# The quadrant sums of W_out in a Winograd feed-forward layer: formed during FFN-out on GpSimd, or during FFN-in on VectorE

## The chip, the cores and the metric

The kernel runs on one core of one Trainium2 chip. The core has a matrix engine (TensorE, in the profile PE, with PEld for its weight loads), VectorE (DVE), ScalarE (ACT), GpSimd (POOL) and SyncE (SP, which only issues transfers here), and 16 DMA engines. Engines run their own instruction streams in order and wait for each other on semaphores. SBUF is the on-chip memory of 128 partitions, PSUM holds what TensorE writes, and DRAM tensors keep what does not fit. The metric is the device time of one execution in microseconds (us), lower is better. A kernel is timed in several runs, and the median counts.

## The reference

One layer of an encoder trunk over 1024 tokens of width 1024, in float32:

```
h = swiglu(rms_norm(x), ffn1_w_in, ffn1_w_out);  x = x + 0.5 * rms_norm(h)
m = token_mixing(rms_norm(x), ...);              x = x + rms_norm(m)
h = swiglu(rms_norm(x), ffn2_w_in, ffn2_w_out);  x = x + 0.5 * rms_norm(h)

def _swiglu(x, w_in, w_out):
    g, u = jnp.split(x @ w_in, 2, axis=-1)      # w_in: 1024 x 5632
    return (jax.nn.silu(g) * u) @ w_out         # w_out: 2816 x 1024
```

Token mixing is a projection, a retention branch and a neighbourhood attention, and three output projections. The change touches the two feed-forward layers, above all the product with `w_out`.

## The kernel before

**Exact float32 from three passes.** Each operand is split into a high part (ScalarE, line 61) and the rest (VectorE, or GpSimd where asked, line 62), and `mm3` (lines 88 to 90) makes three matmuls of a 128x128 by a 128x512 tile: high by high, rest by high, high by rest. So an operand tile of 128x512 needs one ScalarE and one VectorE instruction before TensorE can use it. `piece` splits into a ring of eight wh/wl pairs; `raw` loads 512 KB into the ring `wraw` of three buffers of 4 KB a partition.

**Winograd.** Every large product is cut into 2x2 quadrants and done with seven products in place of eight (`Winograd`, `Pairs`). That needs sums of quadrants of the operands. For the left operand they are called a11, a12, a22, s1 to s4. For the right operand b they are t1 = b12 - b11, t2 = b22 - t1, t3 = b22 - b12 and t4 = b21 - t2.

**FFN-in** (`ffn_in`, `Pairs.run`). 22 pairs of column tiles; one pair is seven products of 12 matmuls. VectorE makes the t sums of the pair's weights, the rests of the splits, the additions of the products out of PSUM and the gate product (line 417); ScalarE makes the high parts and SiLU. After every second pair `LeftFactors` forms the left factors of the following product on GpSimd (line 440), and stores all seven to DRAM tensors `g0...` or `g1...` by GpSimd's DMA queue (`store`, line 68). Six (first layer) or four (second) pairs have two of their seven products done ahead (`lead`); in the first layer three of them wait in six buffers with the tag `lead`.

**FFN-out** (`ffn_out`). Seven products, in the order a11, s1, s2, s3, a22, a12, s4, of 11 steps each. A step takes one 128x512 tile of the left factor (`Blocks`: load `graw`, split into gh and gl) and one of the right operand, and makes 12 matmuls: four token tiles of 128 by three passes. Four PSUM banks gather a product and are taken out by p1 to p7. The left factors sit in two pools, g0 and g1, with four buffers of gh and gl in all.

The right operand is whole in SBUF: twelve tiles `x` of up to four 128x512 blocks hold the four quadrants of `w_out`, loaded on SyncE's queue at the steps of `LOADS`. GpSimd forms the t sums in place, one block at a time (`sub`, line 537; `prepare` puts t1 from step 8, t2 from 19, t3 from 24 and t4, which forms t2 anew, from 30). That is 55 subtractions in each FFN-out. The first four blocks of b11 come as raw loads instead.

After the fourth product GpSimd adds q tiles (lines 571, 572) and ScalarE takes their squares (line 481) for the post-norm. Tokens 0 to 511 are finished during the last two products, tokens 512 to 1023 after them. The residual tiles `xs` are loaded into freed blocks of the quadrants, those of tokens 512 to 1023 of the first layer into the wraw ring (`xload`).

**Between the stages.** The first FFN-out passes its rows to the mixer's projection: norm, transposes on TensorE, and the sums of the next left operand in `Winograd.put`. The mixer's loads and the attention (pools pa, na, ret) follow.

**Order.** Instructions are written in the order of the program; the framework schedules them per engine by that order as priority and puts the waits in. Pools are opened and closed by stage on two stacks, left and right, in SBUF. A pool that lands on bytes of closed pools waits for all of their users before any of its tiles can be used. The scratch for the descriptors of GpSimd's DMA queue has its default size.

Of the kernel before, what the change touches and what calls it, by code (L numbers as in the profile page):

```python
# [10 lines left out]
F32 = mybir.dt.float32  # L11
# [21 lines left out]
LOADS = (0, 2, 4, 6, 9, 12, 14, 17, 20, 23, 26, 29)  # L33
# [371 lines left out]
def ffn_in(c, pairs, pool, put):  # L405

    nc = c.nc
    for i in range(FT):
        gate = [pool.tile([P, 512], F32, tag=f"c{j}", name=f"c{j}", bufs=2) for j in range(2)]
        gt = pool.tile([P, S], F32, tag="gt", name="gt", bufs=3)  # L410
        up = gt[:, :512], gt[:, 512:]

        def done(j):
            if j < 2:
                nc.scalar.activation(gate[j], gate[j], AF.Silu)  # L415
            if j in (1, 2):
                nc.vector.tensor_tensor(up[j % 2], gate[j % 2], up[j % 2], ALU.mult)  # L417
        pairs.run(i, (*gate, *up).__getitem__, done)
        put(i, gt)
# [87 lines left out]
def ffn_out(c, tiles, q, blocks, w_out, gl, ep, side={}):  # L507
# [5 lines left out]
    spare = [t[2][:, 3] for b in tiles for t in b]  # L513
    later, rest, flips, xs = [], [], [], {}

    def quad(k, i, j):
        return tiles[i][j][k // 4][:, k % 4]

    def load(i, j, n):
        m = min(4, NK - 4 * n)  # L520
        nc.sync.dma_start(tiles[i][j][n][:, :m], w_out[2 * i + j][:, n * 2048:n * 2048 + m * 512]
                          .rearrange("p (k f) -> p k f", k=m))

    def xload(t):

        if t < 4 or ep.pre is None:
            tile = (tiles[0][1] + tiles[0][0])[t // 2]
            xs[t] = tile[:, t % 2 * 2:t % 2 * 2 + 2].rearrange("p k f -> p (k f)")
            nc.sync.dma_start(xs[t], ep.resid(t))
        else:  # L530
            xs[t] = c.raw(ep.resid(t))


    order = []

    def sub(out, a, b):
        e = nc.gpsimd.tensor_tensor(out, a, b, ALU.subtract).ins  # L537
        if order:
            c.tc.add_manual_dep(e, order[-1].name, mybir.DependencyInfo(
                mybir.DependencyClass.NoSync, mybir.DependencyReason.DATA), reason="order")  # L540
        order.append(e)

    def t1(k):
        sub(quad(k, 0, 0), quad(k, 0, 1), quad(k, 0, 0))

    def t2(k):
        sub(spare[k % 4], quad(k, 1, 1), quad(k, 0, 0))

    def t3(k):
        sub(quad(k, 0, 1), quad(k, 1, 1), quad(k, 0, 1))  # L550

    def t4(k):
        t2(k)
        sub(quad(k, 0, 0), quad(k, 1, 0), spare[k % 4])
# [11 lines left out]
    def p7(u, b):  # L566
        tt(q[3][:, u], b, q[1][:, u], ALU.add)

        def more():
            xload(u)  # L570
            add(q[1][:, u], q[1][:, u], q[2][:, u], ALU.add)
            add(q[2][:, u], q[3][:, u], q[2][:, u], ALU.add)
            ep.square(u, 1, q[2][:, u], spare[u])
        later.extend((more, None))
# [17 lines left out]
    def p3(u, b):  # L592
        e = tt(q[1][:, u], b, q[1][:, u], ALU.add)
        out = q[1][:, u] if ep.pre is not None else q[3][:, u]
        ep.square(4 + u, 1, q[1][:, u], b if ep.pre is not None else spare[2 + u % 2], out, nc.vector if u == 3 else nc.gpsimd)
# [10 lines left out]
        if u == 2 and 7 not in xs:  # L606
            xload(7)

    def b11(k):
        if k < 4:  # L610
            if k % 2 == 0:
                raws.append(c.raw(w_out[0][:, k * 512:(k + 2) * 512]))
            return raws[-1][:, k % 2 * 512:k % 2 * 512 + 512]
        return quad(k, 0, 0)

    raws = []
    products = (("a11", b11, p1), ("s1", lambda k: quad(k, 0, 0), p5),
                ("s2", lambda k: spare[k % 4], p6), ("s3", lambda k: quad(k, 0, 1), p7),
                ("a22", lambda k: quad(k, 0, 0), p4), ("a12", lambda k: quad(k, 1, 0), p2),
                ("s4", lambda k: quad(k, 1, 1), p3))  # L620
    steps = [(i, k) for i in range(len(products)) for k in range(NK)]
    loads = dict(zip(LOADS, ((0, 0, 1), (0, 0, 2), (0, 0, 0),
                             *((i, j, n) for i, j in ((0, 1), (1, 1), (1, 0)) for n in range(3)))))
    xloads = {n: 4 + j for j, n in enumerate((68, 69, 70) if ep.pre is not None else (59, 62, 65, 68))}
    operands, banks, last = {}, {}, []

    def prepare(n):
        for f, n0 in zip((t1, t2, t3, t4), (8, 19, 24, 30)):
            if 0 <= n - n0 < NK:
                f(n - n0)  # L630
# [9 lines left out]
    for n, (i, k) in enumerate(steps):  # L640
        for m in range(2):
            operand(n + m)
        if n in loads:
            load(*loads[n])
        prepare(n)
# [380 lines left out]
def trunk_layer(ctx: ExitStack, tc, x, g1a, w1i, w1o, g1b, gma, wmt, wnv, wrv, logits, dtab, rope, bias,  # L1026
# [15 lines left out]
    gl = [{n: dt(f"g{i}{n}", [P, FT // 2 * 512]) for n in Winograd.NAMES} for i in range(2)]  # L1042
    x1, x2 = dt("x1", [S, D]), dt("x2", [S, D])
# [13 lines left out]
    def pool(stack, name, side="left"):  # L1057
        return stack.enter_context(tc.tile_pool(name=name, bufs=1, side=side))
# [5 lines left out]
    with tc.tile_pool(name="norm1", bufs=1) as ep:  # L1064
# [10 lines left out]
    g0 = pool(left, "gl10")  # L1075
    with tc.tile_pool(name="fin1", bufs=1) as fp:
        ffn_in(c, fin, fp, LeftFactors(c, early, gl[0]))
    right.close()

    spool = pool(left, "s1")  # L1080
# [3 lines left out]
    wx = Winograd(c, (x0pool, x1pool, spool), None, (4, 4, 2, 8, 8, 8, 8), d["a21"])  # L1084
    ep_stack, g_stack = ExitStack(), ExitStack()
    ep = pool(ep_stack, "ep1")
    g1 = pool(g_stack, "gl11")
    b11, b12, b21, b22 = ([p.tile([P, 4, 512], F32, tag="x", name="x", bufs=n) for p, n in q] for q in (
        ((x0pool, 4),) * 3, ((x1pool, 2), (x1pool, 2), (x0pool, 4)), ((spool, 8),) * 3, ((spool, 8),) * 3))
    q = [p.tile([P, 4, 512], F32, tag="x", name="q", bufs=n) for p, n in ((ep, 2), (ep, 2), (spool, 8), (spool, 8))]  # L1090
    ahead = {}
    fo = Epilogue(c, ep, g1b, gma, rows(x), rows(x1), wx.put)
    rest = ffn_out(c, [[b11, b12], [b21, b22]], q, Blocks(c, (g0, g1, g1, g1), (1, 3)), w1o, gl[0], fo,
                   {n: (lambda j=j: ahead.update({j: c.load_w(wnv[j])})) for j, n in enumerate((65, 66))})
    g_stack.close()
    wx.tmp = pool(g_stack, "cmb1")
# [61 lines left out]
    with tc.tile_pool(name="pa", bufs=1) as pa:  # L1158
# [95 lines left out]
    with tc.tile_pool(name="na", bufs=1) as na:  # L1254
# [3 lines left out]
    with tc.tile_pool(name="ret", bufs=1) as ret:  # L1258
# [50 lines left out]
    with tc.tile_pool(name="ep2", bufs=1) as ep:  # L1309
# [12 lines left out]
    with tc.tile_pool(name="fin2", bufs=1) as fp:  # L1322
        ffn_in(c, fin, fp, LeftFactors(c, cmb, gl[1]))
# [3 lines left out]
    g0, g1, w2 = (pool(right, n, "right") for n in ("gl20", "gl21", "w2"))  # L1327
    tiles = [[[w2.tile([P, 4, 512], F32, tag="x", name="x", bufs=12) for _ in range(3)] for _ in range(2)]
             for _ in range(2)]
    with tc.tile_pool(name="out2", bufs=1) as op:  # L1330
        q = [op.tile([P, 4, 512], F32, tag="q", name="q", bufs=4) for _ in range(4)]
        ffn_out(c, tiles, q, Blocks(c, (g0, g1, g0, g1), (2, 2)), w2o, gl[1],
                Epilogue(c, op, g2b, None, rows(x2), rows(out), None))
# [79 lines left out]
```

## Time and profile before

| what | value |
|---|---|
| time, median of 3 runs | 2327.08 us (2325.92 to 2331.17) |
| span of the profiled execution | 2324.0 us; the page gives no other time of that execution |
| between span and median | 3.1 us |
| TensorE busy | 96% of the span |
| first FFN-in, FFN-out | to 455.4 us; 455.4 to about 692 us |
| second FFN-in, FFN-out | to 2088.0 us; 2088.0 to about 2315 us |

The profile is one execution. A row of a timeline has start, duration, engine, line, operation, output<-input. A row of the groups has line, engine, operation, tiles, shapes, count, then busy us and mean ns of one, then the idle time of the engine just before those instructions and what ended it. A row of the waits says who waited for whom: us in total, times, longest. A row of the chain has start, duration and what ran. A row of the DMA issues has what goes where, the queue, the count, KB of each and the median us from issue to landing. In rows of stretches a pair such as `22.06 (x95)` is busy time and number of instructions. Instructions of VectorE and TensorE overlap a little with the next one, so the distance of two starts is what one takes of the engine's time.

### The profile page before, as it was taken

To read this page: it belongs to the slowest core of one execution; us is meant where nothing else is said; L and a number is where in the kernel's file an instruction comes from. 1 tells how busy PE (TensorE), PEld (TensorE's weight loads), DVE (VectorE), ACT (ScalarE), POOL (GpSimd) and SP (SyncE) were. 2 spreads that over 40 slices of the span, in tenths; PEclk is the share of its full clock that TensorE was granted. 3 is DMA by queue.
4 is the path that set the end of the run, shared out by engine and by line. 5 is a ranking of instruction groups with operands and counts; after the bars stand their busy time and mean duration, and the time that the engine had idled before them with its cause. 6 is when DMAs were issued, how large, how long until landed. Compare 5 with 4: busy or idle time off the path is not lost.

```text
span 2324.0 us, 29917 instructions
## 1 busy us (share of the span) xinstructions
PE 2230.8 (96%) x10288; PEld 1840.8 (79%) x10288; DVE 1742.4 (75%) x2833; ACT 1004.1 (43%) x2102; POOL 744.6 (32%) x735
## 2 busy tenths in 40 slices
PE   6999999999998999999999999999799999999998
PEld 5788888777786887778888888887588888887776
DVE  7886666689778768869875678547887666668966
ACT  6332222343454323248885675226533333224443
POOL 5232222368424134411101222101523131326942
PEclk9999999999998999999999999999899999999999
DMA  4332323374335542257744566766433232328443
GB/s 145 121 137 101 117 95 110 138 275 153 106 114 172 177 159 100 108 177 243 219 164 172 162 219 233 281 219 212 146 114 118 95 114 95 118 92 321 122 130 122
DMA packets 135896, 361.25 MB, mean 155 GB/s; under 512 B 16000, under 2 KB 43776, under 8 KB 133632
## 3 DMA queue, kind: packets, MB, share of 16 engines
q1 hardware_dynamic: 109344, 271.76, 36.1%
q0 software_dynamic: 26400, 87.58, 9.5%
q8 instruction: 81, 1.33, 0.2%
q14 instruction: 71, 0.58, 0.1%
HBM read 263.33 MB, written 100.14 MB: 156 GB/s over the span
## 4 chain that ended last, share of the span: by engine, by line
PE 71%; DVE 13%; issue 7%; POOL 4%; DMA 3%; ACT 3%; POOLq 0%; SPq 0%; DVEq 0%; ACTq 0%
PE ps L90 22%; PE ps L88 22%; PE ps L89 22%; DVE wl L62 3%; DVE gl L62 2%; PE pt L88 1%; PE pt L89 1%; PE pt L90 1%; DMA wraw<-in_dram 1%; DVE tmp L118 1%; POOL rstd L98 1%; DMA x<-in_dram 1%; ACT wh L61 1%; POOL cmb L288 1%; POOL q L482 1%
## 5 line engine op out<-in xcount | busy, mean ns | idle before, releaser
L62 DVE TENSOR_TENSOR wl<-wraw,wh 128x512 fp32r<-128x512 f32 x516 | 381.3, 762 | 80.0 <-ACT wh L61 79.0
L61 ACT CAST wh<-wraw 128x512 fp32r<-128x512 f32 x524 | 300.7, 618 | 205.4 <-PE ps L89 68.2
L90 PE MATMUL ps<-wh,gl 128*128 128x512 f32 x612 | 242.7, 400 | 16.4 <-DVE gl L62 16.0
L88 PE MATMUL ps<-wh,gh 128*128 128x512 f32 x612 | 241.9, 397 | 7.0 <-ACT gh L61 5.8
L89 PE MATMUL ps<-wl,gh 128*128 128x512 f32 x612 | 241.4, 395 | 2.1 <-DVE wl L62 2.1
L62 DVE TENSOR_TENSOR gl<-graw,gh 128x512 fp32r<-128x512 f32 (+2 forms) x178 | 184.3, 1039 | 76.6 <-ACT gh L61 76.4
L61 ACT CAST gh<-graw 128x512 fp32r<-128x512 f32 (+2 forms) x178 | 106.7, 601 | 211.9 <-PE ps L89 68.5
L537 POOL TENSOR_TENSOR x<-x 128x512 f32<-128x512 f32 x110 | 181.0, 1672 | 40.1 <-DMA x<-in_dram 28.9
L415 ACT ACTIVATE c<-c 128x512 f32<-128x512 f32 x88 | 55.7, 633 | 294.7 <-DVE c L385 195.3
L62 DVE TENSOR_TENSOR wl<-x,wh 128x512 fp32r<-128x512 f32 x146 | 168.0, 1161 | 8.2 <-ACT wh L61 8.2
L90 PEld LDWEIGHTS ps<-wh,gl 128*128 128x128 f32 x612 | 116.4, 191 | 51.9 <-DVE gl L62 28.1
L88 PEld LDWEIGHTS ps<-wh,gh 128*128 128x128 f32 x612 | 116.6, 190 | 34.2 <-ACT gh L61 8.9
L89 PEld LDWEIGHTS ps<-wl,gh 128*128 128x128 f32 x612 | 116.8, 191 | 26.9 <-DVE wl L62 3.2
L61 ACT CAST wh<-t 128x512 fp32r<-128x512 f32 x58 | 36.1, 622 | 197.3 <-DVE t L379 196.0
L90 PE MATMUL ps<-a12h,wl 128*128 128x512 f32 x280 | 109.9, 393 | 3.7 <-DVE wl L62 3.7
L88 PE MATMUL ps<-a11h,wh 128*128 128x512 f32 x280 | 111.6, 399 | 1.4 <-ACT wh L61 0.7
L90 PE MATMUL ps<-a11h,wl 128*128 128x512 f32 x280 | 110.5, 395 | 0.7 <-DVE wl L62 0.7
L89 PE MATMUL ps<-a11l,wh 128*128 128x512 f32 x280 | 110.6, 395 | 0.0
L88 PE MATMUL ps<-a12h,wh 128*128 128x512 f32 x280 | 110.3, 394 | 0.0
L68 POOL DMA_DIRECT2D g1a<-gt x33 | 18.1, 550 | 286.3 <-DVE gt L417 286.3
L88 PE MATMUL ps<-a22h,wh 128*128 128x512 f32 x280 | 109.8, 392 | 0.0
L89 PE MATMUL ps<-a12l,wh 128*128 128x512 f32 x280 | 109.2, 390 | 0.0
(359 smaller groups left out, 6197.6 us busy)
## 6 DMA issues: line engine op xcount, KB each, us to landing
wraw<-in_dram SPq DMA_DIRECT2D x221, 512.0 KB, 4.4
x<-in_dram SPq DMA_DIRECT2D x16, 1024.0 KB, 6.9
g0s<-cmb POOLq DMA_DIRECT2D x44, 256.0 KB, 2.5
graw<-g0s SPq DMA_DIRECT2D x44, 256.0 KB, 2.9
g1s<-cmb POOLq DMA_DIRECT2D x44, 256.0 KB, 2.6
graw<-g1s SPq DMA_DIRECT2D x44, 256.0 KB, 3.0
bt<-in_dram SPq DMA_DIRECT2D x24, 384.0 KB, 4.0
g0a<-gt POOLq DMA_DIRECT2D x33, 256.0 KB, 2.3
```

The source lines that it names most:

```text
L61: nc.scalar.copy(h, src)
L62: (eng or nc.vector).tensor_tensor(l, src, hf, ALU.subtract)
L68: self.nc.gpsimd.dma_start(dst, src)
L88: mm(ps, a[0], b[0], start=start, stop=False)
L89: mm(ps, a[0], b[1], start=False, stop=False)
L90: mm(ps, a[1], b[0], start=False, stop=stop)
L98: self.nc.gpsimd.tensor_tensor(r[:, :n], ms, self.mhalf[:, :n], ALU.pow)
L118: nc.vector.scalar_tensor_tensor(xn[:, bs], x[:, bs], r[:, 0:1], gain[:, bs], op0=ALU.mult, op1=ALU.mult)
L288: nc.gpsimd.tensor_tensor(s3, h2, s3, ALU.subtract)
L415: nc.scalar.activation(gate[j], gate[j], AF.Silu)
L482: (eng or c.nc.gpsimd).tensor_tensor(h if out is None else out, h, self.post[:, b * 512:(b + 1) * 512], ALU.mult)
L537: e = nc.gpsimd.tensor_tensor(out, a, b, ALU.subtract).ins
```

## The change

- `OutSums` is new. In FFN-in it loads the four quadrants of `w_out`, one 128x512 block of each, forms t1 to t4 of the block on VectorE and stores them to DRAM tensors `t0...` or `t1...` through GpSimd's queue. `ffn_in` calls it after each of the four results of a pair, from pair 6 (first layer) or 4 (second). The first call of a block issues the loads, the next four one subtraction and one store each: 55 calls for 11 blocks. The buffers are the six of tag `lead` in the first layer, four new ones (`tw`) in the second.
- `ffn_out` has no quadrants in SBUF and no subtractions. `wraw` loads the right operand of two steps at a time, from `w_out` or the stored sums, into the ring `wraw`; the left factors come as before.
- The residual tiles `xs` have buffers of their own and are loaded at steps 30 to 36 and 57 to 63.
- The pools of SBUF named in the diff and all opened by the helper `pool` take `reuse_waits="tile"`: a tile waits only for the users of earlier tiles on its own bytes.
- The pools are laid out anew: in the first FFN-out q, junk, left factors and x tiles lie on the left in the order mid0, gl10, mid1, gl11, mid2, the rest (ep1) on the right; the mixer's pool s1 is opened after them. The scratch for GpSimd's DMA descriptors becomes 4 KB a partition.

```diff
-def ffn_in(c, pairs, pool, put):
+def ffn_in(c, pairs, pool, put, sums):
...
             if j in (1, 2):
                 nc.vector.tensor_tensor(up[j % 2], gate[j % 2], up[j % 2], ALU.mult)
+            sums(i)
...
+class OutSums:
+    def __init__(self, c, tile, src, dst, first):
+        self.first, self.left = first, self.steps(c, tile, src, dst)
+
+    @staticmethod
+    def steps(c, tile, src, dst):
+        tt = c.nc.vector.tensor_tensor
+        for k in range(FT // 2):
+            ks = slice(k * 512, (k + 1) * 512)
+            b11, b12, b21, b22 = b = [tile() for _ in range(4)]
+            for q in range(4):
+                c.nc.sync.dma_start(b[q], src[q][:, ks])
+            yield
+            for n, o, x, y in ((0, b11, b12, b11), (2, b12, b22, b12), (1, b22, b22, b11), (3, b21, b21, b22)):
+                tt(o, x, y, ALU.subtract)
+                c.store(dst[n][:, ks], o)
+                yield
+
+    def __call__(self, i):
+        if i >= self.first:
+            next(self.left, None)
...
-def ffn_out(c, tiles, q, blocks, w_out, gl, ep, side={}):
+def ffn_out(c, q, blocks, junk, xtile, w_out, t_out, gl, ep, side={}):
...
     def xload(t):
-        if t < 4 or ep.pre is None:
...
-            xs[t] = c.raw(ep.resid(t))
+        xs[t] = xtile(t)
+        nc.sync.dma_start(xs[t], ep.resid(t))
...
         def more():
-            xload(u)
             add(q[1][:, u], q[1][:, u], q[2][:, u], ALU.add)
...
+    products = (("a11", w_out[0], p1), ("s1", t_out[0], p5), ("s2", t_out[1], p6), ("s3", t_out[2], p7),
+                ("a22", t_out[3], p4), ("a12", w_out[2], p2), ("s4", w_out[3], p3))
...
+    xloads = {n: j for j, n in enumerate((30, 32, 34, 36, 57, 59, 61, 63))}
+    def wraw(n):
+        if n not in raws:
+            raw = c.wpool.tile([P, D], F32, tag="wraw", name="wraw", bufs=3)
+            (i, k), two = steps[n], n + 1 < len(steps) and steps[n][1] < NK - 1
+            nc.sync.dma_start(raw[:, :512 + 512 * two], products[i][1][:, k * 512:(k + 1 + two) * 512])
+            raws[n] = raw[:, :512]
+            if n + 1 < len(steps):
+                if not two:
+                    nc.sync.dma_start(raw[:, 512:], products[i + 1][1][:, :512])
+                raws[n + 1] = raw[:, 512:]
+        return raws.pop(n)
...
-            operands[n] = blocks(gl[products[i][0]][:, k * 512:(k + 1) * 512]), c.piece(products[i][1](k))
+            operands[n] = blocks(gl[products[i][0]][:, k * 512:(k + 1) * 512]), c.piece(wraw(n))
...
-        return stack.enter_context(tc.tile_pool(name=name, bufs=1, side=side))
+        return stack.enter_context(tc.tile_pool(name=name, bufs=1, side=side, reuse_waits="tile"))
...
-    with tc.tile_pool(name="na", bufs=1) as na:
+    with tc.tile_pool(name="na", bufs=1, reuse_waits="tile") as na:
...
+    mid = ExitStack()
+    m0 = pool(mid, "mid0")
+    q += [m0.tile([P, 4, 512], F32, tag="q", name="q", bufs=2) for _ in range(2)]
+    junk = [m0.tile([P, 512], F32, name=f"junk{u}") for u in range(2)]
+    g0 = pool(mid, "gl10")
+    m1 = pool(mid, "mid1")
+    junk += [m1.tile([P, 512], F32, name=f"junk{u}") for u in range(2, 4)]
+    g1, m2 = pool(mid, "gl11"), pool(mid, "mid2")
+    rest = ffn_out(c, q, Blocks(c, (g0, g0, g0, g1), (3, 1)), junk,
+                   lambda t: (m1, m2, ep, ep)[t // 2].tile([P, D], F32, tag="xs", name="xs", bufs=2 + t // 4 * 2),
+                   w1o, t1o, gl[0], fo,
...
-    nc = _bacc.Bacc("TRN2", target_bir_lowering=False, num_devices=1)
+    nc = _bacc.Bacc("TRN2", target_bir_lowering=False, num_devices=1, dynamic_dma_scratch_size=4096)
```

More of the change, by code (lines that the diff above doesn't have):

```diff
@@ L594, in p3 @@
         out = q[1][:, u] if ep.pre is not None else q[3][:, u]
-        ep.square(4 + u, 1, q[1][:, u], b if ep.pre is not None else spare[2 + u % 2], out, nc.vector if u == 3 else nc.gpsimd)
+        ep.square(4 + u, 1, q[1][:, u], b if ep.pre is not None else junk[2 + u % 2], out, nc.vector if u == 3 else nc.gpsimd)
         g = ep.steps(4 + u, xs[4 + u], (q[0][:, u], out))
@@ L605, in p3 @@
             flips.extend(next(rest[j]) for j in ((), (), (0,), (1, 2, 3))[u])
[L606 to L620, printed above, removed]
-    steps = [(i, k) for i in range(len(products)) for k in range(NK)]
[L622 to L630, printed above, removed]
+    products = (("a11", w_out[0], p1), ("s1", t_out[0], p5), ("s2", t_out[1], p6), ("s3", t_out[2], p7),
+                ("a22", t_out[3], p4), ("a12", w_out[2], p2), ("s4", w_out[3], p3))
+    steps = [(i, k) for i in range(len(products)) for k in range(NK)]
+    xloads = {n: j for j, n in enumerate((30, 32, 34, 36, 57, 59, 61, 63))}
+    operands, raws, banks, last = {}, {}, {}, []
+    def wraw(n):
[9 more added lines that the diff above has]
+        return raws.pop(n)
     def operand(n):
@@ L642, in ffn_out @@
             operand(n + m)
-        if n in loads:
-            load(*loads[n])
-        prepare(n)
         if n == NK:
@@ L1042, in trunk_layer @@
     gl = [{n: dt(f"g{i}{n}", [P, FT // 2 * 512]) for n in Winograd.NAMES} for i in range(2)]
+    t1o, t2o = ([dt(f"t{i}{n}", [P, FT // 2 * 512]) for n in range(4)] for i in range(2))
     x1, x2 = dt("x1", [S, D]), dt("x2", [S, D])
@@ L1074, in trunk_layer @@
         fin.lead(lambda: early.tile([P, 512], F32, tag="lead", name="lead", bufs=6), on_pool=(3, 4, 5, 0))
-    g0 = pool(left, "gl10")
-    with tc.tile_pool(name="fin1", bufs=1) as fp:
-        ffn_in(c, fin, fp, LeftFactors(c, early, gl[0]))
+    with tc.tile_pool(name="fin1", bufs=1, reuse_waits="tile") as fp:
+        ffn_in(c, fin, fp, LeftFactors(c, early, gl[0]),
+               OutSums(c, lambda: early.tile([P, 512], F32, tag="lead", name="lead", bufs=6), w1o, t1o, 6))
     right.close()
-    spool = pool(left, "s1")
     x0pool = pool(right, "x0", "right")
@@ L1083, in trunk_layer @@
     x1pool = pool(x1_stack, "x1", "right")
-    wx = Winograd(c, (x0pool, x1pool, spool), None, (4, 4, 2, 8, 8, 8, 8), d["a21"])
+    wx = Winograd(c, (x0pool, x1pool, None), None, (4, 4, 2, 8, 8, 8, 8), d["a21"])
     ep_stack, g_stack = ExitStack(), ExitStack()
[L1086 to L1090, printed above, removed]
-    ahead = {}
-    fo = Epilogue(c, ep, g1b, gma, rows(x), rows(x1), wx.put)
-    rest = ffn_out(c, [[b11, b12], [b21, b22]], q, Blocks(c, (g0, g1, g1, g1), (1, 3)), w1o, gl[0], fo,
+    ep = pool(ep_stack, "ep1", "right")
+    fo = Epilogue(c, ep, g1b, gma, rows(x), rows(x1), wx.put)
+    q = [ep.tile([P, 4, 512], F32, tag="q", name="q", bufs=2) for _ in range(2)]
+    ahead = {}
+    mid = ExitStack()
[9 more added lines that the diff above has]
+                   w1o, t1o, gl[0], fo,
                    {n: (lambda j=j: ahead.update({j: c.load_w(wnv[j])})) for j, n in enumerate((65, 66))})
-    g_stack.close()
-    wx.tmp = pool(g_stack, "cmb1")
+    mid.close()
+    spool = pool(left, "s1")
+    wx.pools.update({n: spool for n in ("s1", "s2", "s3", "s4")})
+    wx.tmp = pool(g_stack, "cmb1", "right")
     a21 = []
@@ L1157, in trunk_layer @@
     ep_stack.close()
-    with tc.tile_pool(name="pa", bufs=1) as pa:
+    with tc.tile_pool(name="pa", bufs=1, reuse_waits="tile") as pa:
         evpool[:] = [pa]
@@ L1257, in trunk_layer @@
     fill.until("rv")
-    with tc.tile_pool(name="ret", bufs=1) as ret:
+    with tc.tile_pool(name="ret", bufs=1, reuse_waits="tile") as ret:
         ret_cores(c, ret, mix, d, dec, fill, RET_FILL)
@@ L1308, in trunk_layer @@
     wx.s3_on_pool = (4, 5)
-    with tc.tile_pool(name="ep2", bufs=1) as ep:
+    with tc.tile_pool(name="ep2", bufs=1, reuse_waits="tile") as ep:
         rest = c.out_proj(KT, stream(c, gs, lambda k: d["m"][k]), lambda k: c.load_w(wmo[k]),
@@ L1319, in trunk_layer @@
             f()
-    with tc.tile_pool(name="fin2", bufs=1) as fp:
-        ffn_in(c, fin, fp, LeftFactors(c, cmb, gl[1]))
+    tw = pool(left, "tw2")
+    with tc.tile_pool(name="fin2", bufs=1, reuse_waits="tile") as fp:
+        ffn_in(c, fin, fp, LeftFactors(c, cmb, gl[1]),
+               OutSums(c, lambda: tw.tile([P, 512], F32, tag="tw", name="tw", bufs=4), w2o, t2o, 4))
     left.close()
@@ L1326, in trunk_layer @@
     g_stack.close()
[L1327 to L1333, printed above, removed]
+    g0 = pool(right, "gl20", "right")
+    op = pool(left, "out2")
+    q = [op.tile([P, 4, 512], F32, tag="q", name="q", bufs=4) for _ in range(4)]
+    fo = Epilogue(c, op, g2b, None, rows(x2), rows(out), None)
+    g1 = pool(left, "gl21")
+    jp = pool(left, "junk2")
+    junk = [jp.tile([P, 512], F32, name=f"junk{u}") for u in range(4)]
+    ffn_out(c, q, Blocks(c, (g0, g1, g0, g1), (2, 2)), junk,
+            lambda t: jp.tile([P, D], F32, tag="xs", name="xs", bufs=8), w2o, t2o, gl[1], fo)
+    left.close()
     right.close()
```

32 lines of the change are left out of this document (2 added, 30 removed).

## The prediction

> **What bounds the kernel now.** I read the page first, then the waits of TensorE, then the stages around the change as stretches of time.
>
> ```profile
> PE 2230.8 (96%) x10288; PEld 1840.8 (79%) x10288; DVE 1742.4 (75%) x2833; ACT 1004.1 (43%) x2102; POOL 744.6 (32%) x735
> 160.00:440.00 280.00, 280.00 (x1237) 231.94 (x1236) 193.52 (x299) 85.69 (x151) 69.97 (x82) 1.00 0.30 105
> ```
>
> The first row is the page's, the second is most of the first FFN-in (width, then busy time and count of PE, PEld, DVE, ACT, POOL, then granted clock, DMA share, GB/s). TensorE is the bound: 1237 matmuls fill 280 us, so a fed matmul takes 280/1237 = 0.2264 us. The change removes no matmul. All it can win is time in which TensorE is not fed; all it can lose is feeding it worse. FFN-in has no such time now. FFN-out has; it begins at 455.4 and at 2088.0:
>
> ```profile
> 455.40:480.00 24.60, 22.06 (x95) 17.26 (x94) 14.10 (x18) 9.66 (x18) 11.22 (x13) 1.00 0.96 373
> 480.00:500.00 20.00, 17.53 (x75) 13.55 (x74) 20.00 (x16) 11.28 (x21) 16.28 (x11) 1.00 0.65 227
> 500.00:540.00 40.00, 40.00 (x178) 33.15 (x177) 39.96 (x29) 19.16 (x34) 35.55 (x22) 1.00 0.62 216
> 540.00:580.00 40.00, 36.47 (x147) 27.93 (x147) 40.00 (x31) 13.70 (x24) 35.85 (x22) 0.96 0.45 132
> 600.00:620.00 20.00, 16.77 (x72) 12.92 (x72) 13.95 (x18) 9.78 (x19) 5.70 (x4) 1.00 0.37 106
> 2088.00:2100.00 12.00, 9.44 (x34) 7.02 (x33) 9.21 (x10) 4.56 (x8) 8.13 (x10) 0.86 0.93 340
> 2120.00:2180.00 60.00, 59.57 (x263) 49.00 (x262) 58.85 (x44) 29.09 (x52) 51.16 (x31) 1.00 0.60 200
> 2180.00:2206.00 26.00, 22.91 (x89) 17.17 (x88) 26.00 (x20) 8.19 (x15) 25.37 (x17) 0.93 0.51 139
> 2220.00:2240.00 20.00, 16.77 (x68) 12.65 (x67) 12.62 (x12) 8.62 (x20) 16.06 (x12) 0.95 0.24 69
> ```
>
> I take each stretch's width less 0.2264 us for each matmul in it as lost. First FFN-out: 24.6 - 95 x 0.2264 = 3.1; then 3.0; 0 (178 matmuls fill the 40 us); 6.7; and 3.7 at 600 to 620. Second: 4.3; 0.5; 5.9; and 4.6 at 2220 to 2240. VectorE is busy 40.00 of 40.00 in the stretch that loses most, and POOL 35.85.
>
> **Why VectorE is the late one there.** By groups, 476 to 577 us, then two rows of VectorE's timeline from that stretch and two from behind it:
>
> ```profile
> L62 DVE TENSOR_TENSOR wl<-x,wh 128x512 fp32r<-128x512 f32 x33 | 52.1, 1590 | 4.7 <-ACT wh L61 4.7
> L62 DVE TENSOR_TENSOR gl<-graw,gh 128x512 fp32r<-128x512 f32 x32 | 47.8, 1504 | 0.0
> L537 POOL TENSOR_TENSOR x<-x 128x512 f32<-128x512 f32 x55 | 90.8, 1678 | 20.9 <-DMA x<-in_dram 14.8 <-DVE wl L62 5.2
> ...
> 543.38 1.78 DVE L62 TENSOR_TENSOR wl<-x,wh 128x512 fp32r<-128x512 f32 x1
> 545.08 1.77 DVE L62 TENSOR_TENSOR gl<-graw,gh 128x512 fp32r<-128x512 f32 x1
> 579.43 0.68 DVE L62 TENSOR_TENSOR gl<-graw,gh 128x512 fp32r<-128x512 f32 x1
> 580.03 0.68 DVE L62 TENSOR_TENSOR wl<-x,wh 128x512 fp32r<-128x512 f32 x1
> ```
>
> The same subtraction is issued every 1.70 us while POOL subtracts, and every 0.60 us once POOL's 55 are over. A step of FFN-out is 12 matmuls, 12 x 0.2264 = 2.72 us, and needs two of them: 3.40 us against POOL, 1.20 us without it. So VectorE falls 0.68 us behind in each step that POOL covers, eats up the operands held ahead, and then TensorE waits for it.
>
> **Part 1: no POOL subtractions in FFN-out.** All 55 of line 537 go, from each FFN-out. With 1.20 us of 2.72 needed, VectorE cannot be late there: the losses at 480 to 500, 540 to 580, 2120 to 2180 and 2180 to 2206 go, 3.0 + 6.7 + 0.5 + 5.9 = 16.1 us. Bounds 12 (a quarter stays, as the clock after a stall, 0.96 and 0.93 above) to 16.1. I take 16.1.
>
> **Part 2: the start of FFN-out.** Two rows of SyncE's queue beside TensorE's last FFN-in matmul of the second layer:
>
> ```profile
> 455.70 0.33 SPq L456 DMA_DIRECT2D graw<-g0a  x1
> ...
> 2087.85 0.39 PE L90 MATMUL ps<-s4h,wl 128*128 128x512 f32 x1
> 2088.31 0.33 SPq L456 DMA_DIRECT2D graw<-g1a  x1
> ```
>
> The left factors' loads beyond the first buffer wait for the end of FFN-in, since their pool lies on its pools; that is the 3.1 and the 4.3 us. After, the first three buffers of the first FFN-out (pool gl10, above 16 KB of q and 4 KB of junk, as much as FFN-in's pool held) lie outside FFN-in's pool, and in the second gl21 does the same; the products' right operands come through the wraw ring, which no stage owns. Taken off: 7.4 us (bounds 3 to 7.4).
>
> **Part 3: the sums move to VectorE in FFN-in.** 44 subtractions a layer instead of 55 on POOL, one at each of four of five calls of `sums`, from pair 6 (4 in the second layer). 160 to 440 us by groups, VectorE's three groups with idle time before them, and POOL's additions:
>
> ```profile
> L390 DVE TENSOR_TENSOR c<-ps,gt 128x512 f32<-128x512 f32 x15 | 10.4, 692 | 30.4 <-PE ps L90 30.4
> L385 DVE TENSOR_TENSOR c<-ps,c 128x512 f32<-128x512 f32 x14 | 9.7, 692 | 26.1 <-PE ps L90 26.1
> L382 DVE TENSOR_TENSOR gt<-ps,c 128x512 f32<-128x512 f32 x14 | 9.7, 692 | 27.3 <-PE ps L90 17.5 <-POOL cmb L440 9.7
> L440 POOL TENSOR_TENSOR cmb<-gt 128x512 f32<-128x512 f32 x14 | 23.6, 1707 | 7.4 <-DVE gt L417 7.4
> L440 POOL TENSOR_TENSOR cmb<-gt,cmb 128x512 f32<-128x512 f32 x15 | 19.6, 1310 | 0.3
> ```
>
> A pair is 84 matmuls, 19.0 us; 280 us hold 14.7. VectorE idles 30.4 + 26.1 + 27.3 = 83.8 us there, 5.7 us a pair, nearly all of it waiting for TensorE. A k of the sums spans five calls, 1.25 pairs, 7.1 us of idle; its four subtractions cost 4 x 0.60 = 2.4 us clean and 4 x 1.70 = 6.8 us if POOL is at each (it is for 43.2 of 280 us). Both fit, so TensorE pays nothing for them. Without that cover, 88 x 0.60 = 53 us.
>
> Their DMAs: 44 loads of 256 KB on SyncE's queue and 44 stores on POOL's, in each FFN-in.
>
> ```profile
> wraw<-in_dram SPq DMA_DIRECT2D x221, 512.0 KB, 4.4
> x<-in_dram SPq DMA_DIRECT2D x16, 1024.0 KB, 6.9
> g0s<-cmb POOLq DMA_DIRECT2D x44, 256.0 KB, 2.5
> graw<-g0s SPq DMA_DIRECT2D x44, 256.0 KB, 2.9
> SPq L72 <- DVE wl L62: 285.3, 32, 17.4
> L68 POOL DMA_DIRECT2D g0s<-cmb x31 | 17.0, 550 | 0.0
> ```
>
> (The last two are the queue's wait for a free wraw buffer, 150 to 440 us, and POOL's time for an issue.) 23 MB in some 300 us are 77 GB/s on top of 105, under the 373 moved at 455 us. A load put behind a blocked wraw load on SyncE is late; then the subtraction waits on VectorE, and behind it PSUM's evacuations and the wl pieces for TensorE. A store waits on POOL for its subtraction, and behind it the additions of line 440 and their stores; POOL is busy 70 of 280 us, and 3.2 stores a pair add 1.8 of 19 us. I charge 2 us for both layers, bounds 0 and 10 (half a microsecond on each of 22 k).
>
> **Part 4: FFN-out streams both operands.** The twelve quadrant loads of 768 KB to 1 MB of each FFN-out go. Each step loads 256 KB of left and 256 KB of right operand: 0.524 MB in 2.72 us, 193 GB/s, where 216 at a DMA share of 0.62 did not slow TensorE (500 to 540 us). Four left buffers are 10.9 us ahead against a landing of 2.9, three wraw buffers hold six steps. Cost 0.
>
> The Trainium skill speaks against this part: "DMA: Bandwidth & Descriptors", section "Bandwidth", asks for transfers of 1 MiB or more, and streaming replaces loads of 768 KB and 1 MB by ones of 256 and 512 KB. The rows agree for one transfer by itself (256 KB in 2.9 us, 1024 KB in 6.9), but not for several in flight (373 GB/s at 455 us). What it would cost alone is the third rival.
>
> **Part 5: x tiles, pools, scratch.** The mixer's start, waits and chain:
>
> ```profile
> PE ps L741 <- ACT qh L64: 3.7, 1, 3.7
> 1030.03 4.73 DMA sn<-ev
> 1034.87 4.56 DMA kraw<-nk
> ...
> 701.85 4.16 DMA wraw<-in_dram
> 706.70 1.22 PE ps L88 x2
> ```
>
> The kraw load was issued when the last store of the pool before it had landed, though it needs none of its data. Waiting by tile, it can start earlier: 0 to 3.7 us, I take 3. At 701.85 a weight load waited for a wraw buffer that held an x tile; x tiles get their own buffers, so up to 4.85 us (701.85 to 706.70) earlier. VectorE is nearly full there, so I take 2 (0 to 4.85). The smaller DMA scratch: no row shows a POOL queue that waits for room; at worst a store waits for the one ahead to land, 2.5 us, off TensorE's path. 0.
>
> **What stays**: 3.7 and 4.6 us at 600 to 620 and 2220 to 2240. POOL's additions after the fourth product hold up ScalarE, whose next gh TensorE needs:
>
> ```profile
> 602.73 1.70 POOL q L572
> 605.71 1.38 DVE gl L62
> ACT x L481 <- POOL q L572: 11.1, 4, 4.1
> ```
>
> These instructions are the same after, so I leave it in.
>
> **Sum.** 16.1 + 7.4 + 3 + 2 - 2 = 26.5 us. The page's span is 2324.0 us, the median 2327.08; the 3.1 us between lie around the span and stay. 2327.1 - 26.5 = 2300.6, say **2300.5 us**. Own range: gain 12 + 3 - 10 = 5 at worst, 16.1 + 7.4 + 3.7 + 4.85 = 32 at best, so 2295 to 2322.
>
> **Rivals.**
> 1. *Slower: FFN-in bound by VectorE.* If the four loads of a k are issued only shortly before the first subtraction, VectorE waits for 1 MB, 6.9 us by the x row. A k has 7.1 us of idle and 2.4 go to its subtractions: 4.7 are left, so 2.2 us a k fall on TensorE, 22 x 2.2 = 48 us; 2327.1 - 28.5 + 48 = 2347 us. It decides from a wait of 4.7 + 28.5/22 = 6.0 us. For it: the 285.3 us that SyncE's queue is blocked. Against: the loads need no result, and buffers are free a call ahead.
> 2. *More: the stall behind POOL's additions goes too*, as VectorE enters that stretch with all buffers full: another 8.3 us, 2292 us. For it: in the first layer those buffers had been drained up to 577 us. Against: the operands are at most four steps, 10.9 us, ahead, and ScalarE waits 11.1 us in all, with two gaps close together.
> 3. *Slower by far: streaming one transfer at a time.* 2.9 + 4.4/2 = 5.1 us a step against 2.72: 2.4 x 154 steps = 370 us, about 2670 us. Against: the 373 GB/s.
> 4. *It does not do what it says:* the pools still wait, and the sums' cost in FFN-in eats part 1: 2327 us.
>
> **How the numbers follow.** The forecast has 0.67, the second rival 0.17, the first 0.09, the third 0.02, the fourth 0.05. A measurement of this kernel tells 0.2%, 4.7 us, from no change. Faster 0.84 (forecast and second), same 0.05, slower 0.11. The range leaves out the slower cases and part of the second rival: 2285 to 2322.
>
> **What would show it.** Right: no line 537 on POOL; FFN-out's gl and wl at 0.68 us up to the fourth product; about 209 us (924 x 0.2264) plus the additions' stall and the transposes for each FFN-out; left-factor loads issued before FFN-in's last matmul; FFN-in still 1237 matmuls in 280 us with VectorE some 10% busier. Wrong: in FFN-in, TensorE waiting for VectorE, and VectorE for loads of line `src[q]`; in FFN-out, TensorE waiting behind DMA; or the two stalls behind POOL's additions gone or grown.

## The result: slower, 2360.5 us

The changed kernel takes 2360.51 us (median of 4 runs, 2356.13 to 2363.65) against 2326.5 us for the kernel before in the same session: ratio 1.0143, 95% interval 1.0128 to 1.0159, so 34 us slower where 26.5 us faster had been forecast. The page of its profiled execution:

```profile
span 2361.9 us, 30397 instructions
PE 2240.7 (95%) x10288; PEld 1846.2 (78%) x10288; DVE 1704.5 (72%) x2921; ACT 1001.7 (42%) x2102; POOL 626.7 (27%) x713
```

VectorE and GpSimd (POOL) have less to do than before (1742.4 and 744.6 us), and TensorE does the same 10288 matmuls. By stretches of time (columns as in the prediction):

```profile
160.00:440.00 280.00, 263.03 (x1124) 214.90 (x1124) 204.66 (x311) 76.55 (x136) 97.49 (x117) 0.97 0.49 171
520.00:580.00 60.00, 60.00 (x266) 49.69 (x266) 28.85 (x46) 29.13 (x52) 0.00 (x0) 1.00 0.66 205
1700.00:1920.00 220.00, 202.85 (x849) 163.08 (x850) 182.22 (x268) 65.87 (x116) 80.08 (x99) 0.96 0.59 200
```

In FFN-out, at 520 to 580 us, TensorE is fed without a gap: what was to be won there was won. The loss is where nothing was lost before, in FFN-in. The first has 1124 matmuls in 280 us instead of 1237: 113 x 0.2264 = 25.6 us. The second loses 27.8 us in 220, against this row of the kernel before (972 - 849 = 123 matmuls):

```profile
1700.00:1920.00 220.00, 220.00 (x972) 182.22 (x971) 163.55 (x254) 71.14 (x126) 57.48 (x67) 1.00 0.33 113
```

VectorE is not full there, 204.66 of 280 us. What ended the waits, 100 to 310 us of the changed kernel (waiter, then who ended it: us in total, times, longest), and below it the group of the sums in the same stretch:

```profile
POOL t L67 <- DVE lead L524: 59.5, 22, 8.3
DVE lead L524 <- DMA lead<-in_dram: 38.8, 8, 7.9
PE ps L89 <- DVE wl L61: 16.6, 7, 6.6
```

```profile
L524 DVE TENSOR_TENSOR lead<-lead 128x512 f32<-128x512 f32 x44 | 33.3, 771 | 39.0 <-DMA lead<-in_dram 38.8
```

All 44 subtractions of the first layer lie in this stretch: 33.3 us of work and 39.0 us in which VectorE stood before one of them until a load had landed. The timeline shows what that does:

```profile
213.04 1.90 DVE L386 TENSOR_TENSOR wraw<-wraw 128x512 f32<-128x512 f32 x1
222.83 0.69 DVE L524 TENSOR_TENSOR lead<-lead 128x512 f32<-128x512 f32 x1 [7.90 <-DMA lead<-in_dram]
223.44 0.69 DVE L392 TENSOR_TENSOR gt<-ps,c 128x512 f32<-128x512 f32 x1
224.04 0.68 DVE L393 TENSOR_TENSOR gt<-ps,gt 128x512 f32<-128x512 f32 x1
224.64 0.68 DVE L61 TENSOR_TENSOR wl<-t,wh 128x512 fp32r<-128x512 f32 x1
...
225.38 0.79 PE L89 MATMUL ps<-s2h,wl 128*128 128x512 f32 x1 [6.56 <-DVE wl L61]
```

The engine takes its instructions in order. For 7.90 us a subtraction whose result is first read in FFN-out, over 260 us later, stands at the head; behind it stand two evacuations of PSUM and the wl piece, and TensorE waits 6.56 us for that piece. The chain of waits shows where such a load is late:

```profile
233.44 0.54 POOL t L67
...
235.24 7.32 DMA t<-lead
...
242.57 4.02 DMA lead<-in_dram
...
246.71 0.69 DVE lead L524
```

A store of a sum takes 7.32 us to land; only then may the next load overwrite its buffer, which takes 4.02 us; only then does the next subtraction run.

The program calls for the sums from the 7th to the 20th pair. In the compiled order of VectorE's queue they stand elsewhere (counted from VectorE's timelines; a pair ends with its last addition out of PSUM):

```
subtractions placed by the end of pair    3   6   7   8  10  12  13  20
changed kernel                            0   4   9  17  30  43  44  44
run "paced" (below)                       0   0   4   7  13  20  23  44
```

So the framework puts a subtraction far ahead of the place of its call, in an order that is fixed before the kernel runs. Why it does so is not shown: I take it that it reckons with times at which the operands ought to be ready, and goes as early as a buffer allows. On the chip the stores and loads were not done by then.

A second loss is the start of the first FFN-out. Two stretches, then SyncE's queue (SPq), ScalarE and TensorE:

```profile
480.00:500.00 20.00, 14.84 (x66) 11.96 (x64) 12.69 (x15) 5.93 (x10) 8.71 (x10) 0.93 0.71 239
500.00:520.00 20.00, 15.05 (x54) 12.14 (x55) 5.25 (x9) 5.18 (x9) 0.00 (x0) 0.73 0.82 290
```

```profile
496.55 0.84 SPq L456 DMA_DIRECT2D graw<-g0a  x2
504.28 0.62 ACT L60 CAST gh<-graw 128x512 fp32r<-128x512 f32 x1 [8.49 <-DMA graw<-g0a]
504.95 0.79 PE L87 MATMUL ps<-wh,gh 128*128 128x512 f32 x1 [10.11 <-ACT gh L60]
```

TensorE stops for 10.11 us after three steps. The missing left factor is the fourth step's; in SyncE's order its load (the second of the two in the row of SyncE's queue) stands behind those of six later steps, as its buffer is the one that lies on FFN-in's pool. It was issued at 496.92 and landed at 504.18 us, 7.3 us later.

### The profile page after: what moved, and what is told of

The parts are those of the page before. It is cut to its first block, busy times and chain, and to the rows that moved or that the text cites. A ratio compares the mean times of both kernels' runs of the same rounds, so it can differ in the third digit from the quotient of the medians.

```text
span 2361.9 us, 30397 instructions
## 1 busy us (share of the span) xinstructions
PE 2240.7 (95%) x10288; PEld 1846.2 (78%) x10288; DVE 1704.5 (72%) x2921; ACT 1001.7 (42%) x2102; POOL 626.7 (27%) x713
## 4 chain that ended last, share of the span: by engine, by line
PE 63%; DVE 13%; issue 8%; POOL 8%; DMA 6%; ACT 2%; SPq 0%; POOLq 0%; DVEq 0%; ACTq 0%
PE ps L89 19%; PE ps L87 19%; PE ps L88 19%; DVE wl L61 2%; POOL cmb L440 2%; PE pt L87 1%; PE pt L88 1%; PE pt L89 1%; POOL rstd L97 1%; PE ps L721 1%; PE pt L740 1%; DMA t<-tw 1%; POOL t L67 1%; DMA graw<-g0a 1%; DMA t<-lead 1%
## 5 line engine op out<-in xcount | busy, mean ns | idle before, releaser
L61 DVE TENSOR_TENSOR wl<-wraw,wh 128x512 fp32r<-128x512 f32 x662 | 491.9, 764 | 81.3 <-ACT wh L60 80.2
L60 ACT CAST wh<-wraw 128x512 fp32r<-128x512 f32 x670 | 391.1, 617 | 244.5 <-PE ps L88 84.3
L61 DVE TENSOR_TENSOR gl<-graw,gh 128x512 fp32r<-128x512 f32 (+2 forms) x178 | 130.9, 736 | 188.8 <-ACT gh L60 188.6
L89 PE MATMUL ps<-s2h,wl 128*128 128x512 f32 x232 | 97.5, 420 | 21.4 <-DVE wl L61 21.4
L89 PE MATMUL ps<-a22h,wl 128*128 128x512 f32 x280 | 109.1, 390 | 0.0
L88 PE MATMUL ps<-a22l,wh 128*128 128x512 f32 x280 | 109.0, 389 | 0.0
```

The costliest lines, as they stand in the source:

```text
L60: nc.scalar.copy(h, src)
L61: (eng or nc.vector).tensor_tensor(l, src, hf, ALU.subtract)
L88: mm(ps, a[0], b[1], start=False, stop=False)
L89: mm(ps, a[1], b[0], start=False, stop=stop)
```

## The experiments

The theory (A): the place of the sums in VectorE's queue costs the time in FFN-in, not their work or their bytes. Its rivals: the left factors that FFN-out reads back early, or DMA traffic in general (B); no room on VectorE (C); the loop of buffers and queues, whichever engine subtracts (D).

**no_sums**

```diff
-        if i >= self.first:
-            next(self.left, None)
+        return
...
-w1o, t1o, gl[0], fo,
+w1o, w1o, gl[0], fo,
```

(and the same for w2o.)

> The 44 subtractions a layer, their loads and stores are left out of FFN-in, and FFN-out multiplies with plain quadrants of W_out in their place, so the output is not the reference's; everything else of the change stays. Theory A (VectorE's queue stands behind the loads of the sums): both FFN-in phases get back what they lost to them, some 25 us in the first and 22 in the second, so 2310 to 2320 us; the first FFN-in keeps the 6 us lost behind the early left factors. Theory B (the losses in FFN-in come from the left factors of FFN-out that are read back early, or from more DMA traffic in general): 2345 us or more, with the matmul counts at 180 to 300 us still low.

Measured: 2307.96 us, 0.9921 [0.9906, 0.9936] of the kernel before.

```profile
160.00:440.00 280.00, 280.00 (x1237) 231.82 (x1237) 197.17 (x301) 85.36 (x151) 75.75 (x86) 1.00 0.32 111
```

FFN-in is full again, and 52.5 us come back, against 25.6 + 27.8 = 53.4 counted above. The early left factors are still there, so that half of B falls. The sums' own DMA traffic is gone too (111 GB/s instead of 171), so traffic in general is not yet excluded; the next run does that.

**paced**

```diff
-                tt(o, x, y, ALU.subtract)
+                c.pairs.behind(tt(o, x, y, ALU.subtract))
```

(`c.pairs` is set at the start of `ffn_in`; `behind` is the pairs' own ordering edge.)

> The same instructions as the changed kernel, but each subtraction is ordered on VectorE behind the last addition of line 389's kind (the one after s3's product) of the pair at which the program calls for it, so that the 44 spread over the pairs instead of standing as early as buffers come free. Theory A (the place in VectorE's queue costs the time, not VectorE's work nor the bytes): 2310 to 2325 us, and VectorE's wait for the loads falls from 39 us to under 5. Rival C (VectorE has no room for 44 subtractions of 0.6 to 1.7 us in FFN-in, wherever they stand): 2345 us or more.

Measured: 2309.44 us, 0.9932 [0.9917, 0.9947]. Two stretches, then the group of the sums, 100 to 460 us:

```profile
160.00:440.00 280.00, 280.00 (x1237) 231.84 (x1236) 216.18 (x344) 84.90 (x150) 108.14 (x131) 1.00 0.54 188
1700.00:1920.00 220.00, 220.00 (x973) 182.15 (x972) 176.96 (x282) 72.00 (x126) 78.52 (x96) 1.00 0.53 185
```

```profile
L525 DVE TENSOR_TENSOR lead<-lead 128x512 f32<-128x512 f32 x44 | 30.7, 704 | 0.0
```

The same 44 subtractions, loads and stores, more VectorE work in the stretch (216.18 us) and more traffic (188 GB/s), and no wait before any of them; TensorE has all its 1237 matmuls. (In the second layer three waits are left, 3.6 us in all.) An ordering edge on each subtraction takes 51 us off the changed kernel, and the sums then cost 1.5 us in all against no_sums, within the uncertainty. A holds; C and the rest of B fall. SyncE's queue still waits for landed stores in this run, without harm:

```profile
SPq L522 <- DMA t<-lead: 64.8, 17, 10.8
POOL t L67 <- DVE lead L525: 65.0, 19, 11.9
```

**pool_sums**

```diff
-        tt = c.nc.vector.tensor_tensor
+        tt = c.nc.gpsimd.tensor_tensor
```

> The subtractions of the sums run on GpSimd instead of VectorE, in the same phase, with the same loads, stores and buffers, as early as buffers come free. Theory A: VectorE no longer waits for the loads of the sums, so FFN-in is fed again: 2310 to 2330 us; GpSimd's own queue waits instead, which reaches TensorE only through the gt buffers that its additions free. Rival D (the loop of load, subtraction, store and landing with its DMA queues delays TensorE through SyncE's queue, whichever engine subtracts): 2345 us or more, TensorE waiting for wl or wh pieces whose weights came late.

Measured: 2389.42 us, 1.0274 [1.0254, 1.0294]; the expectation of A missed by 60 us. The reason is a third one that neither theory had named. VectorE's groups, 140 to 260 us:

```profile
L61 DVE TENSOR_TENSOR wl<-wraw,wh 128x512 fp32r<-128x512 f32 x29 | 38.7, 1359 | 0.0
L416 DVE TENSOR_TENSOR gt<-c,gt 128x512 f32<-128x512 f32 x10 | 18.1, 1811 | 0.1
...
L392 DVE TENSOR_TENSOR gt<-ps,c 128x512 f32<-128x512 f32 x5 | 3.4, 680 | 0.0
...
L393 DVE TENSOR_TENSOR gt<-ps,gt 128x512 f32<-128x512 f32 x5 | 3.4, 676 | 0.0
```

VectorE waits for no sum any more, but its operations with both inputs in SBUF take 1.36 and 1.81 us beside GpSimd's (0.76 and 0.68 in no_sums, same groups and stretch), those with one input in PSUM 0.68. VectorE is busy 111.94 of these 120 us, and TensorE gets 364 matmuls where 530 would fit. The Trainium skill, "SBUF — State Buffer", section "Who interferes with whom", says this: a VectorE instruction with two SBUF inputs contends with a GpSimd instruction that reads SBUF, one with at most one such input does not; the rows agree. So this run moves the old price of FFN-out into FFN-in. Its time lies where D expected it, but for this other reason, so it says nothing for or against D. Two other rows speak against D: paced has the same loads and stores, spread over more pairs, without harm; and in the changed kernel, at 100 to 310 us, VectorE waited for loads of the sums for 38.8 us and for weight loads (wraw) for 2.3.

**bufs8**

```diff
-name="tw", bufs=4)
+name="tw", bufs=8)
```

> The changed kernel with 8 instead of 4 buffers for the sums of the second layer. Theory G (the waits come from the short loop: a buffer's store must land before its next load is issued): the 24 us lost in the second FFN-in fall to half or less: 2340 to 2350 us. Rival H (what counts is that a subtraction stands in VectorE's queue ahead of work that TensorE needs, and the order takes any free buffer as leave to go earlier): 2354 us or more.

Measured: 2368.01 us, 1.0179 [1.0165, 1.0192]. Second FFN-in:

```profile
1700.00:1920.00 220.00, 202.86 (x868) 165.19 (x867) 182.98 (x274) 66.41 (x118) 86.39 (x108) 0.96 0.58 207
```

```profile
DVE tw L524 <- DMA tw<-in_dram: 12.3, 3, 7.6
PE ps L89 <- DVE wl L61: 8.7, 2, 7.2
```

VectorE waits less often (12.3 us in 3 waits, 21.4 in 9 in the changed kernel), but 104 matmuls, 23.5 us, are still missing in the stretch, where G wanted half or less of the loss. Rival H holds: more buffers let the order go earlier still (42 of the 44 subtractions stand before the end of the seventh pair, 30 in the changed kernel), and one wait of 7.6 us on VectorE is one of 7.2 on TensorE. That the time even rose is another matter: at the start of the second FFN-out TensorE waits 7.96 us for a left factor, which it does not in the changed kernel. No run shows why.

**late**

```diff
-                nc.scalar.activation(gate[j], gate[j], AF.Silu)
+                c.silu = nc.scalar.activation(gate[j], gate[j], AF.Silu).ins
...
-        self.c.split(*a, r)
+        with self.c.tc.issue_after(self.c.silu):
+            self.c.split(*a, r)
...
-            nc.sync.dma_start(raw[:, :512 + 512 * two], products[i][1][:, k * 512:(k + 1 + two) * 512])
+            c.load = nc.sync.dma_start(raw[:, :512 + 512 * two], products[i][1][:, k * 512:(k + 1 + two) * 512]).ins
...
-        nc.sync.dma_start(xs[t], ep.resid(t))
+        with c.tc.issue_after(c.load):
+            nc.sync.dma_start(xs[t], ep.resid(t))
...
-            ep.gains()
+            with c.tc.issue_after(c.load):
+                ep.gains()
```

> The sums stay as in the changed kernel. The first left factors of FFN-out are ordered on ScalarE behind FFN-in's last Silu, and FFN-out's x tiles and gains are ordered on SyncE behind the weight load of their own step. Theory A: of the first FFN-in the 6 us at 120 to 160 us come back, of the start of the first FFN-out (13.6 us lost at 480 to 520 us) some 8 to 10 us; the sums' cost stays: 2342 to 2350 us. Theory B (the early left factors are the main cause in FFN-in): 2325 us or less.

Measured: 2349.65 us, 1.0102 [1.0087, 1.0117]. The sum came out, but by luck, as one of its parts did not:

```profile
140.00:160.00 20.00, 20.00 (x90) 16.53 (x89) 19.25 (x33) 7.90 (x14) 4.04 (x7) 1.00 0.64 211
...
480.00:500.00 20.00, 8.57 (x29) 6.57 (x29) 7.08 (x7) 3.63 (x8) 5.53 (x8) 0.66 0.68 230
```

The matmuls at 140 to 160 us are back (75 in the changed kernel), but the start of FFN-out still loses 61 of 90. Keeping the x tiles away did not help it, which led to the next pair. What made up for it lies later in the first FFN-in, 1160 matmuls at 160 to 440 us instead of 1124, where the order of the sums shifted too; this run doesn't separate the two.

**paced_start** and **paced_start_late**: paced, with

```diff
-        p = self.pools[self.n % len(self.pools)]
+        p = self.pools[0 if self.n < self.only else self.n % len(self.pools)]
...
-Blocks(c, (g0, g0, g0, g1), (3, 1))
+Blocks(c, (g0, g0, g0, g1), (3, 1), 8)
```

and in the second of them the `issue_after(self.c.silu)` of late.

> The paced sums, and in the first FFN-out the first 8 steps take their left factors from the three buffers that lie outside FFN-in's pool, where the fourth step took the one that lies on it. Theory E (the 13 to 14 us lost at the start of the first FFN-out are the fourth step's left factor, whose load stands on SyncE behind six later ones): the loss falls to 3 us or less and the time to 2296 to 2301 us. Rival F (the x tiles and gains that load there fill the DMA engines): the loss stays, 2306 to 2312 us.

> The same, and the left factors' high parts are ordered on ScalarE behind FFN-in's last Silu. Theory: the 4 to 5 us that TensorE loses at 100 to 160 us, behind left factors read back while they are being stored, come back as well: 2291 to 2297 us. If those waits had been hidden, or come again at the start of FFN-out because the first factors are then split late: no less than the run before.

Measured: 2299.02 us, 0.9880 [0.9867, 0.9894], and 2292.62 us, 0.9859 [0.9843, 0.9874]. First paced (the loss), then paced_start, then paced_start_late:

```profile
455.00:500.00 45.00, 34.04 (x139) 27.62 (x138) 20.08 (x27) 13.15 (x23) 8.71 (x10) 0.85 0.78 269
```

```profile
100.00:160.00 60.00, 58.09 (x254) 47.12 (x253) 51.53 (x76) 19.68 (x34) 18.92 (x23) 1.00 0.48 167
440.00:500.00 60.00, 59.92 (x264) 49.12 (x263) 35.23 (x51) 25.75 (x46) 9.26 (x11) 1.00 0.79 285
```

```profile
100.00:160.00 60.00, 60.00 (x267) 49.67 (x266) 50.50 (x77) 19.62 (x35) 22.97 (x27) 1.00 0.51 182
440.00:500.00 60.00, 60.00 (x267) 49.62 (x265) 35.19 (x51) 27.05 (x49) 8.62 (x10) 1.00 0.81 293
500.00:580.00 80.00, 80.00 (x354) 66.25 (x353) 43.94 (x66) 34.88 (x63) 5.31 (x4) 1.00 0.63 202
580.00:620.00 40.00, 34.55 (x148) 27.10 (x146) 25.80 (x36) 20.18 (x44) 20.06 (x16) 1.00 0.50 161
2180.00:2220.00 40.00, 36.77 (x159) 29.28 (x158) 25.11 (x31) 17.21 (x34) 17.31 (x12) 1.00 0.54 176
```

paced misses 45/0.2264 - 139 = 60 matmuls at the start of FFN-out, 13.5 us; with its fourth step's left factor out of FFN-in's pool that is gone while x tiles and gains still load there, so E holds and F falls. The last 13 matmuls at 100 to 160 us come with the late split; they are 2.9 of the 6.4 us between the two medians, and the rest is not taken apart. TensorE is now fed without a gap from 100 to 580 us (1237 matmuls at 160 to 440), across the seam between FFN-in and FFN-out.

**before_pools** and **before_scratch**: the kernel before with `reuse_waits="tile"` on the pools and the 4 KB scratch, and with the scratch alone.

> The kernel before with only the pools' tile-wise waits and the 4 KB scratch of the change. The prediction's part 5: the neighbourhood attention starts some 3 us earlier: 2322 to 2324 us. Rival: nothing is gained, since what follows there is filled from other work, or earlier loads collide: 2326 us or more.

> The kernel before with only the 4 KB DMA scratch. If all of the gain of the tile-wise pools with the scratch (2317.5 us against 2326.7) is the pools': 2324 to 2329 us. If the scratch has a share, for example by other waits on GpSimd's queue: 2322 us or less.

Measured: 2317.46 us, 0.9960 [0.9947, 0.9972], and 2325.23 us, 0.9996 [0.9986, 1.0005]. The scratch alone makes no difference clear of noise; so the pools' waits give the 9.3 us [6.5, 12.3], three times what I took for the mixer's start. First and last starts of two groups, kernel before, then before_pools:

```profile
L61 ACT CAST k<-kraw x16: 604/617/634, 1039.5 to 1124.7; 64x512 fp32r<-64x512 f32 x16
L61 ACT CAST kh<-kraw x8: 606/616/622, 1227.5 to 1392.7; 128x512 fp32r<-128x512 f32 x8
```

```profile
L61 ACT CAST k<-kraw x16: 602/617/634, 1035.5 to 1119.3; 64x512 fp32r<-64x512 f32 x16
L61 ACT CAST kh<-kraw x8: 607/616/620, 1220.1 to 1385.4; 128x512 fp32r<-128x512 f32 x8
```

4.0 us are won by the start of the neighbourhood attention and 7.4 by that of the retention. Some of the 4.0 is older than the mixer: at 480 to 500 us, in the first FFN-out, before_pools has 84 matmuls where the kernel before has 75, 2.0 us.

**paced_start_late_add**

```diff
-    tt, add = nc.vector.tensor_tensor, nc.gpsimd.tensor_tensor
+    tt = add = nc.vector.tensor_tensor
```

> The run paced_start_late with the two additions per token tile after the fourth product on VectorE instead of GpSimd. The prediction left 3.7 and 4.6 us there as a loss that stays, because ScalarE waits for those GpSimd additions ahead of TensorE's next left factor. If that reading is right: 5 to 9 us less, 2284 to 2288 us. If VectorE, with eight more operations and the left factors' low parts behind them, is late itself, or TensorE then waits for the transposes' work anyway: 2290 us or more.

Measured: 2284.71 us, 0.9821 [0.9808, 0.9834], the fastest version.

```profile
580.00:620.00 40.00, 37.72 (x170) 30.87 (x170) 33.05 (x47) 21.39 (x48) 14.51 (x11) 1.00 0.57 182
2180.00:2220.00 40.00, 40.00 (x178) 33.13 (x177) 32.10 (x44) 21.67 (x46) 12.80 (x9) 1.00 0.55 172
```

22 and 19 matmuls more than the rows of paced_start_late above, 9.3 us by the count and 7.9 by the medians. Two things changed at once here, and the run does not separate them: ScalarE no longer waits for GpSimd's additions (11.2 us in four waits at 570 to 640 us of paced_start_late), and VectorE's splits no longer run beside them (at 575 to 625 us a wl takes 750 ns instead of 901).

## Why the prediction was wrong, step by step

**Part 3 failed**, at the sentence "Both fit, so TensorE pays nothing for them." The sum behind it was right: paced fits the same work into the same idle time for 1.5 us. What was wrong is the step from room to no cost: idle time on an in-order engine is only of use to an instruction that is ready when it reaches the head. I took the sums to stand where the program calls for them, one in each of four of five calls; they stand between the third and the thirteenth pair, close behind loads that must first wait for a store to land. The 2 us charged were 53.4 by the rows and 52.5 by no_sums. The prediction's own sign of being wrong, TensorE waiting for VectorE and VectorE for the loads of the sums, is what the rows show. That the price without any cover, 88 x 0.60 = 53 us, comes out at the same figure is chance: VectorE's work on the sums did fit, the waits did not.

The first rival named this mechanism (VectorE waiting for the loads) and came nearest, 2347 us; it got 0.09 because of "buffers are free a call ahead", the same mistake. Its threshold was a mean wait per k; in fact few waits did it, five of 4.9 to 7.9 us between 160 and 310 us. I take each to have used up the pieces that TensorE had ahead; shown is that every 20 us from 180 to 300 us are short of matmuls (81, 83, 53, 68, 57 and 83 of 90).

**Part 2 was right in the second layer and lost in the first.** The early buffers do start FFN-out without a gap (the second one in the changed kernel, with 104 matmuls in the 23 us from 2137; the first one in paced_start_late), but in the changed kernel the wait moved three steps on: the first FFN-out's start lost 3.1 + 3.0 us before, and 480 to 520 us of the changed kernel holds 120 matmuls, 40 - 120 x 0.2264 = 12.8 us lost. I had counted the three buffers that became free and not the fourth that did not. And loads that may start early also do: left factors split in FFN-in held ScalarE's and VectorE's queues there. At 120 to 160 us the changed kernel lacks 25 matmuls, 5.7 us; 15 of them, 3.4 us, are missing in no_sums too and are the left factors' share. The other 10 came back without the sums, the first of which made VectorE wait 3.65 us for its load, up to 120.35 us.

**Part 1 was right**: 266 matmuls in 60 us at 520 to 580. **Part 4 was right**: at 440 to 500 us of paced_start_late, 293 GB/s of streamed operands, x tiles and gains leave TensorE full. **Part 5** was mis-sized: 9.3 us for the pools, where I took 3 + 2 for pools and x tiles together; the scratch's 0 was right. **What stays** had the right cause, the additions on GpSimd: 8.3 us were named, 7.9 came back once they left it; whether by ScalarE's wait alone stays open.

Put together: 2326.5 - 16.1 - 7.4 - 9.3 + 53.4 + 12.8 + 5.7 = 2365.6 us, 5 above the measured 2360.5. The rows are of one execution, and that one took 2363.65 us, 3 of the 5. The rest is within what is counted twice or wrongly: 2.0 us of the pools' 9.3 lie at 480 to 500 us and are also in the 16.1, and up to 10 of the 123 matmuls of the second FFN-in, 2.3 us, are missing at the seam ahead of it (80 matmuls at 1700 to 1720 us; the kernel before has such a stretch 20 us earlier, with 82). Without the three losses the sum is 2293.7, and paced_start_late took 2292.62; so close a fit is partly luck.

## What to carry to other kernels

Work put into an engine's idle time needs two proofs: that it fits, and that it is ready when it reaches the head of the in-order queue; read the compiled order, not the program's, before counting on the second. Where an instruction that depends on a DMA is not urgent, tie it behind an instruction of its intended place: here an ordering edge on each of 88 subtractions was worth 51 us, and more buffers were worth nothing. When a pool is moved out from under another, look for the one buffer that still lies there: its load may queue behind all that no longer wait.

## What the runs showed of the hardware

Loads and stores of 256 KB landed in 2.9 and 2.5 us (medians) in the kernel before, and took 8.1 (a left factor's load in paced, below) and 7.3 us (a sum's store, above) when others were in flight (269 GB/s at 455 to 500 us of paced): a median over the whole kernel is no bound for a full stretch. And a stop of several us costs TensorE more than its length. After the 10.96 us wait at the start of FFN-out in paced, the chain shows matmuls at 0.43 us each for 5 us, where they had taken 0.23:

```profile
454.91 0.23 PE ps L87
...
471.30 8.08 DMA graw<-g0a
...
480.94 0.43 PE ps L88
...
485.21 0.43 PE ps L89
```

The granted clock of that stretch, 455 to 500 us, was 0.85. This is part of the loss in FFN-in too: at 160 to 440 us of the changed kernel, 1124 matmuls keep TensorE busy for 263.03 us and would need 1124 x 0.2264 = 254.5, so by this count, which rests on the profile's modelled ends of matmuls, some 8.5 of the 25.6 us are slow matmuls behind the stops, and 17 are the stops. The granted clock there was 0.97.
